# Layer 1's values and gates by seven half-size products over pairs of row tiles and column blocks, with weight operands formed and stored in layer 0

## The chip, the core and the metric

The kernel runs on one core of one Trainium2 chip. The metric is the device time of one execution, in microseconds (us). A core has a matrix engine (TensorE, in profiles PE), VectorE (DVE), ScalarE (ACT), GpSimd (POOL) and SyncE (SP), which here only issues transfers. Each engine works through its own list of instructions in order; semaphores tie the lists together. Matrix products accumulate in PSUM, everything else lives in SBUF, and DMA moves data to and from HBM.

## What is computed

A backbone of two layers over 2048 latent tokens and 256 context tokens of width 1024. Layer 0 mixes latent attention and gated linear attention; layer 1 is a 2-D neighbourhood attention. The change concerns layer 1's input projection:

```python
def odd_mixer(h, hc, w_in, q_gain, k_gain, rpb, w_out, update_ctx):
    def heads(u):
        bsz, n, _ = u.shape
        q, k, v, z = jnp.split(u, 4, axis=-1)
        sh = lambda t: t.reshape(bsz, n, C_HEADS, C_HD)
        return rms_norm(sh(q), q_gain), rms_norm(sh(k), k_gain), sh(v), z

    q_x, k_x, v_x, z_x = heads(jnp.dot(h, w_in))
    q_c, k_c, v_c, z_c = heads(jnp.dot(hc, w_in))
    o = neighborhood_attention(q_x, k_x, v_x, k_c, v_c, rpb)
    y = jnp.dot(o.reshape(h.shape[0], h.shape[1], C_WIDTH) * jax.nn.silu(z_x), w_out)
```

`w_in` is 1024 x 4096, with 1024 columns each for queries, keys, values and gates. All is in float32.

## The kernel before

**Tiles and precision.** Tokens stand in 18 row tiles of 128 (tiles 0 and 1 are context), the width in 8 blocks of 128 (`k`), the columns of layer 1's projection in 8 blocks of 512 (`j`: 0, 1 queries; 2, 3 keys; 4, 5 values; 6, 7 gates). A float32 product is made of three matmuls: every operand is split into a high part (rounded to the engine's format by an ACT copy) and a low part (the rest, by a subtraction), and high x high, high x low and low x high are summed (`mm3_steps`, L134 to L136). A *cell* is one row tile by one column block: 8 blocks of `k` x 3 = 24 matmuls of 512 columns into one PSUM bank.

**Stages.** `even_latent` and `even_rest` make layer 0's projections, `even_mix` its attention and output, `odd_qk` layer 1's queries and keys, `odd_vz` its values and gates, `odd_tail` its attention and output. `even_rest` weaves its cells with layer 0's row maxima; weights of its first blocks are split by steps in `self.ahead`, one of which `pump` issues at every fourth step of the main work.

**`odd_qk`** transposes and modulates each row tile (`prep`, `modulate`), stores it in `H` for later and runs the cells of j = 2, 3, 0, 1, three banks in turn. `fin` transposes, scales and stores a cell's result later. Whenever a column block is used up, the next stage's block is loaded and split in its place (`od_steps`: `wraw`, an ACT copy, a DVE subtraction), as steps that `turn` takes. The last three tiles run block by block, with the first value cells of j = 4 at the end; one tile's parts are kept in `HL`.

**`odd_vz`** runs the other value and gate cells, tile by tile: `reload` brings a tile from `H` and splits it again (ACT `hhi`, DVE `hlo`). A value cell is copied out by ACT (`ovz`) and stored by two GpSimd DMAs (`store_v`, L1619). A gate cell takes a tanh on ACT, a multiply-add on DVE (L1649), four transposes (L1652), an ACT copy (`ozt`) and an ACT DMA. `weave` interleaves these 24-matmul cells with `maxes`, upper bounds of each head's scores: per head 16 *items*, each a context matmul (L1704, two items share a bank and a DVE reduction, L1706) and a window matmul (L1711) that DVE adds to a bias table and reduces (L1715). After the 16 items of a head `row` transposes the result (L1668), ACT copies it (`mr`) and four GpSimd DMAs store it in `M` (L1672). Tables (`mtab`), keys (`mk`) and queries (`mq`) come by SP.

**What sets the order.** The program is written in the order that the generators give; `weave(main, side, ratio, lag, head)` takes `ratio` items for each step of the main work and ties a step to an item `lag` back. The framework then orders each engine's list by a simulated schedule, so that instructions can stand in another order than written. A tile's buffer is reused as soon as the last reader in its list is done; DMA issues wait on their queue for that, and hold back what is behind them.

**The seven products.** Layer 0's and layer 1's output projections already use this form (`seven`, L1359): for two row tiles and two column blocks, with the width cut into two halves, the four results come of seven half-width products instead of eight; sums and differences of the blocks stand in their operands, and partial sums pass from one product to the next in the same bank.

## Time and profile before

| | |
|---|---|
| median of 3 runs | 3512.95 us (3510.87 to 3515.46) |
| the profiled execution | 3515.51 us, span 3513.7 us |
| granted clock of the span | 0.994 |
| DMA traffic | 518.00 MB, mean 147 GB/s |
| stages in the span | even_rest about 555 to 1095, odd_qk about 2075 to 2507, odd_vz about 2507 to 2966 us |

Times of day in views are us from the start of the span. A row of a group has line, engine, operation, names out<-in, shapes and count, then busy time and mean length, then the engine's idle time just before and what ended it. A matmul's own length (some 0.4 us for 512 columns) includes the pipeline's depth; its cost to TensorE is the spacing to the next one. Line L111 is a helper through which all of ACT's copies go.

### The profile page before, as it was taken

The page shows a single profiled execution, that of the slowest core. Times are in us where ns is not written, and L with a number is a line of the kernel's source. Part 1 is how long each engine was busy: PE and PEld are TensorE (multiplying, and loading weights), DVE is VectorE, ACT ScalarE, POOL GpSimd, SP SyncE. Part 2 cuts the span into 40 slices and gives each one's busy share as a digit, 9 for nine tenths or more (in the row PEclk, how much of TensorE's full clock was granted, in tenths as well). Part 3 has the DMA queues.
Part 4 walks back from the last instruction along what each step waited for, and adds up shares of the span by engine and source line. Part 5 has one row for each costly group of instructions (what it writes and reads, how often), then busy time and mean ns, then how long its engine had stood idle before and what let it go on. Part 6 is the DMA issues. An engine that isn't in the chain of part 4 may idle for free.

```text
span 3513.7 us, 54120 instructions
## 1 busy us (share of the span) xinstructions
PE 3433.5 (98%) x20228; PEld 2652.7 (75%) x20228; DVE 2350.5 (67%) x3853; ACT 1466.1 (42%) x2612; POOL 1057.8 (30%) x1309
## 2 busy tenths in 40 slices
PE   8999998999999999999999999999999999999899
PEld 6898987888887666665556888888888887555577
DVE  4677756888886777768886655545576663566765
ACT  5445542111113554546664344445422222555632
POOL 1343331111111334332210123333211112787711
PEclk9999999999999999999999999999999999999999
DMA  7555555232325242333634664444766556655374
GB/s 255 144 161 159 148 141 160 96 106 81 103 81 162 62 139 71 102 115 121 179 113 122 131 172 151 152 154 144 262 185 185 179 181 207 222 191 188 120 189 62
DMA packets 354714, 518.00 MB, mean 147 GB/s; under 512 B 33178, under 2 KB 233578, under 8 KB 347492
## 3 DMA queue, kind: packets, MB, share of 16 engines
q1 hardware_dynamic: 301972, 396.55, 37.4%
q0 software_dynamic: 29456, 82.14, 8.9%
q10 hardware_dynamic: 23024, 35.85, 2.9%
q8 instruction: 159, 2.61, 0.3%
q14 instruction: 103, 0.84, 0.1%
HBM read 335.63 MB, written 196.60 MB: 151 GB/s over the span
## 4 chain that ended last, share of the span: by engine, by line
PE 83%; DVE 5%; DMA 5%; ACT 2%; issue 2%; POOL 2%; SPq 1%; ACTq 0%; DVEq 0%; POOLq 0%
PE gm L136 10%; PE gm L134 10%; PE st L1178 10%; PE gm L135 10%; PE av L1088 7%; PE mx L708 4%; PE st L1798 4%; PE o L1828 2%; PE pu L1367 2%; PE o L1367 2%; PE o L1810 1%; PE st L1367 1%; PE pj L1367 1%; PE mx L1711 1%; PE up L127 1%
## 5 line engine op out<-in xcount | busy, mean ns | idle before, releaser
L709 DVE TENSOR_REDUCE mm<-mx 128x1 f32<-128x512 f32 (+1 forms) x656 | 389.2, 628 | 85.2 <-PE mx L708 78.1
L111 ACT ACTIVATE apt<-st 128x1024 f32<-128x1024 f32 (+1 forms) x296 | 300.1, 1014 | 305.9 <-PE st L1178 285.9
L1185 DVE TENSOR_TENSOR acc<-acc,apt 128x1024 f32<-128x1024 f32 x256 | 340.7, 1331 | 83.0 <-ACT apt L111 64.3
L1178 PE MATMUL st<-aq,akh 64*128 64x512 f32 x1728 | 312.7, 410 | 1.0 <-ACT apt L111 0.6
L1088 PE MATMUL av<-apt,av 128*64 128x512 f32 x1152 | 265.8, 598 | 0.0
L708 PE MATMUL mx<-mk,mq 96*128 96x512 f32 (+1 forms) x656 | 236.1, 373 | 5.4 <-DMA mq<-QC 5.4
L1834 POOL TENSOR_TENSOR oacc<-oacc,opt 128x528 f32<-128x528 f32 (+6 forms) x192 | 220.6, 1170 | 44.6 <-ACT opt L111 40.3
L1178 PE MATMUL st<-aq,akl 64*128 64x512 f32 (+1 forms) x1152 | 230.9, 392 | 0.0
L111 ACT ACTIVATE u<-gm 128x352 f32<-128x352 f32 (+1 forms) x140 | 68.5, 496 | 374.9 <-PE gm L136 206.0
L1178 PEld LDWEIGHTS st<-aq,akh 64*128 64x128 f32 x1728 | 153.2, 186 | 83.1 <-ACT apt L111 28.0
L1980 DVE TENSOR_TENSOR opt<-st,tab 128x496 f32<-128x496 f32 (+16 forms) x288 | 124.3, 484 | 117.3 <-PE st L1798 116.9
L1715 DVE CUSTOM_DVE_ANT_0 mx<-mx,mtab 128x465 f32<-128x465 f32 (+7 forms) x256 | 137.2, 542 | 75.0 <-PE mx L1711 70.3
L1088 PEld LDWEIGHTS av<-apt,av 128*64 128x64 f32 x1152 | 76.3, 136 | 135.3 <-issue 134.3
L111 ACT ACTIVATE opt<-opt 128x930 f32<-128x930 f32 (+7 forms) x130 | 104.5, 805 | 133.0 <-DVE opt L1980 124.5
L708 PEld LDWEIGHTS mx<-mk,mq 96*128 96x128 f32 x656 | 121.7, 189 | 17.3 <-issue 5.8
L1178 PEld LDWEIGHTS st<-aq,akl 64*128 64x128 f32 (+1 forms) x1152 | 112.2, 185 | 23.9
L1706 DVE TENSOR_REDUCE mm<-mx 128x2 f32<-128x512 f32 x128 | 88.2, 689 | 45.4 <-PE mx L1704 43.6
L223 POOL TENSOR_TENSOR oss<-oss,mhalf 128x8 f32<-128x8 f32 x68 | 112.3, 1652 | 5.4
L134 PE MATMUL gm<-w1h,hhi 128*128 128x512 f32 x280 | 112.2, 401 | 0.0
L1555 DVE TENSOR_TENSOR onat<-gm,oss 128x512 f32<-128x512 f32 x68 | 46.9, 690 | 95.7 <-POOL oss L223 95.7
L136 PE MATMUL gm<-w1h,hlo 128*128 128x512 f32 x280 | 110.1, 393 | 0.0
L135 PE MATMUL gm<-w1l,hhi 128*128 128x512 f32 x280 | 109.7, 392 | 0.0
(778 smaller groups left out, 9557.0 us busy)
## 6 DMA issues: line engine op xcount, KB each, us to landing
H<-x ACTq DMA_DIRECT2D x32, 512.0 KB
adaw<-ada_w SPq DMA_DIRECT2D x64, 256.0 KB
wraw<-w_od SPq DMA_DIRECT2D x64, 256.0 KB
K1t<-okt POOLq DMA_DIRECT2D x16, 1024.0 KB, 6.6
x<-H SPq DMA_DIRECT2D x31, 512.0 KB
mtab<-rpb_q SPq DMA_DIRECT2D x16, 585.0 KB
x<-xin SPq DMA_DIRECT2D x18, 512.0 KB
x<-xin POOLq DMA_DIRECT2D x18, 512.0 KB, 5.2
```

What stands on the lines that cost most here:

```text
L111: return self.nc.scalar.activation(out, in_, func, **kw)
L134: self.nc.tensor.matmul(out, lh(k), rh(k), start=start and j == 0, stop=False)
L135: self.nc.tensor.matmul(out, lh(k), rl(k), start=False, stop=False)
L136: yield self.nc.tensor.matmul(out, ll(k), rh(k), start=False, stop=stop and j == n - 1)
L708: mm = nc.tensor.matmul(ps[:, :w], q[:A_QK, (t % 6) * P : (t % 6) * P + P], k[:A_QK, k0 : k0 + w], start=True, stop=True)
L709: nc.vector.tensor_reduce(out=m[:, t, n : n + 1], in_=ps[:, :w], axis=AX.X, op=ALU.max)
L1088: mm = nc.tensor.matmul(O[j, nb][i * 64 : i * 64 + 64, :w], V[j, kt // TT][:, kt % TT, i * 64 : i * 64 + 64], pts[:, i, :w], start=n == 0, ...
L1178: mm = nc.tensor.matmul(ps[:, o // 64, :w], k[o : o + r, kb, kq], Q[o : o + r, qb, :w], start=m == 0, stop=m == 4)
L1185: added = nc.vector.tensor_tensor(out=acc[:, :, :w], in0=a[:, :, :w], in1=pts[:, :, :w], op=ALU.add)
L1367: self.mm = self.nc.tensor.matmul(ps, x[:, k, :], y, start=start and k == 0 and n == 0, stop=k == self.H4 - 1 and n == 2, skip_group_check ...
L1798: mm = nc.tensor.matmul(ps(i), ones[s] if k is None else k[s, ks], qs(q[s]), start=n == 0, stop=n == 3)
L1834: nc.gpsimd.tensor_tensor(out=a, in0=a, in1=pts[:, :, a0 - r0 : a1 - r0, :], op=ALU.add)
```

## The change

Row tiles t and t+1, the two column blocks of the values (or of the gates) and the two halves of the width form a *unit*: 9 units of values (18 tiles) and 8 of gates (16 tiles), 7 products of 12 matmuls each.

- **Weight operands.** Seven *parts* for the values and seven for the gates (sums and differences of the blocks, split into high and low) are formed in `even_rest` by `sum_steps`, appended to `self.ahead`: per step of 256 columns 4 SP loads, 11 GpSimd operations, 7 ACT copies and 7 GpSimd stores to `Tw`, 16 times in all (176, 112 and 112; 29.4 MB are stored). The splitting of blocks 4 to 7 in layer 1 goes. `weight_part` loads a ready part (128 x 4096, 2.1 MB) into the place of a weight.
- **Row operands.** `operand(n, i)` forms the operand of product i of unit n: up to one GpSimd sum or difference, an ACT copy (high) and a GpSimd subtraction (low); 7 and 11 operations of 512 columns a unit. They are written after product i of the unit before. `pair_load` brings the two tiles from `H` by SP (three loads, 1 MB) after products 5 and 6.
- **`odd_qk`** has no value cells any more; the last two tiles run block by block, and unit 0 (values of tiles 0 and 1) at the end, with the remaining `fin`. Parts 0 to 6 of the values are loaded as slots come free: one after j = 0, two each after 1, 2 and 3. `HL` goes.
- **`odd_vz`** runs units 1 to 8 (values) and 9 to 16 (gates), woven with `maxes` at 0.64 items per step of three matmuls, head 16 (before 0.615, 32). Unit 8 loads gate part i after its product i. Three of a unit's results need a DVE addition; gates are transposed later (`flip`). `mx` has 4 banks instead of 5.

```diff
+    def sum_steps(self, f, sp):
...
+        for k in range(self.H4):
+            for c in (slice(0, 256), slice(256, 512)):
...
+                def split(n, x):
+                    y = self.tl(sp, [P, 2, 256], "tsp", F32R, bufs=2)
+                    self.act(y[:, 0, :], x[:])
+                    dif(y[:, 1:2, :].rearrange("p z c -> p (z c)"), x, y[:, 0:1, :].rearrange("p z c -> p (z c)"))
+                    g.dma_start(self.Tw[f, n, :, :, k, c], y[:].bitcast(F32))
...
@@ even_rest
+            self.ahead += [self.held(self.sum_steps(f, sp)) for f in range(2)]
...
@@ odd_qk
-            nxt = {2: 4, 3: 5, 0: 6, 1: 7}
-            done = lambda j: j in nxt and self.later.append(self.od_steps(win, nxt[j], ws, lambda: self.done))
...
+                for i in {0: (0,), 1: (1, 2), 2: (3, 4), 3: (5, 6)}[j]:
+                    self.weight_part(0, i, ws)
+                if j == 0:
+                    self.later.append(self.operand(0, i) for i in range(4))
+            cells = self.cells(list(range(NT - 2)), (2, 3, 0, 1), lambda t, j: j > 1 or t >= NCT, 1, 0)
+            cells += [(t, j) for j in range(4) for t in (NT - 2, NT - 1)]
...
+    PARTS = [(2, "h"), (3, "h"), (3, "l"), (0, "h"), (0, "l"), (1, "h"), (1, "l")]
...
+    def weight_part(self, f, i, ws):
+        n, z = self.PARTS[i]
+        x = self.pw[i] = self.tl(ws[n // 2], [P, 2, self.H4, 512], f"w{n}{z}", F32R, bufs=1)
+        self.wload = self.nc.sync.dma_start(x[:].bitcast(F32), self.Tw[f, i])
...
+    def operand(self, n, i):
...
+        if i in before:
+            o, x, y, op = before[i]
+            g.tensor_tensor(out=o, in0=x, in1=y, op=op)
+        x = (a[0], t, t, a[1], b[0], a[1], b[1])[i]
+        hi, lo = self.ops[i]
+        self.act(hi, x)
+        g.tensor_tensor(out=lo, in0=x, in1=hi, op=ALU.subtract)
+        if i > 4:
+            self.pair_load(n + 1, (i - 5,))
+    def unit(self, n, banks, place, result, ws):
...
+        for i, ps in enumerate((U, V, U, W, U, V, U)):
+            w, op = self.pw[i], self.ops[i]
+            for k in range(self.H4):
+                for m, (x, y) in enumerate(((0, 0), (0, 1), (1, 0))):
+                    mm = self.nc.tensor.matmul(ps, op[x][:, k, :], w[:, y, k, :], start=i in (0, 1, 3) and k == 0 and m == 0,
+                                               stop=k == self.H4 - 1 and m == 2, skip_group_check=True)
+                yield mm
+            if i < 3:
+                kept[(3, 4, 5)[i]] = x = place()
+                self.done = self.act(x, ps)
+            else:
+                row, c = {3: (0, 0), 4: (1, 1), 5: (0, 1), 6: (1, 0)}[i]
+                result(t + row, c, ps, kept.pop(i, None), place)
+            if swap:
+                self.weight_part(1, i, ws)
+            self.operand(n + 1, i)
...
@@ odd_vz
-            self.weave(gemms, maxes(), 0.615, 15, 32)
+            self.weave(gemms(), maxes(), 0.64, 15, 16)
```

The change moves instructions at three places that the prediction speaks of. Rows show line, operation, out<-in with the tile's numbers, shape and the semaphores waited for (lines of the changed kernel where it is its list).

TensorE in `odd_vz` before: products of a cell (`gm`) stand one to four at a time between maxes items (`mx`).

```order
L135 MATMUL gm_27092<-w3l_23682,hhi_26622 128x512
L136 MATMUL gm_27092<-w3h_23681,hlo_26623 128x512
L134 MATMUL gm_27092<-w3h_23681,hhi_26622 128x512
L1711 MATMUL mx_26925<-mk_26485,mz_4058_23643 128x288 [waits DVE_49]
L135 MATMUL gm_27092<-w3l_23682,hhi_26622 128x512
```

TensorE in `odd_vz` now, within one of the two longest bunches: between a product on part w3l (`sv` is a unit's bank, L1713 its matmul) and one on w1h stand 10 items; L1843 and L1850 are the former L1704 and L1711. This is the end of the bunch.

```order
L1843 MATMUL mx_25721<-mk_25683,mz_4218_24265 128x256 [waits DVE_49]
L1850 MATMUL mx_25723<-mk_25683,mz_4218_24265 128x352 [waits DVE_49]
L1850 MATMUL mx_25738<-mk_25683,mz_4218_24265 128x264 [waits DVE_49]
L1843 MATMUL mx_25747<-mk_25683,mz_4219_24266 128x256 [waits DVE_49,Activation_49]
L1850 MATMUL mx_25749<-mk_25683,mz_4219_24266 128x360 [waits DVE_49]
L1850 MATMUL mx_25760<-mk_25683,mz_4219_24266 128x480 [waits DVE_49]
L1713 MATMUL sv_25705<-w1h_24087,hlo_24092 128x512 [waits Activation_49]
L1807 MATMUL mx_25773<-ident_58,mc_25681 16x128 [waits DVE_49]
L1713 MATMUL sv_25704<-w3l_23901,w2l_23791 128x512 [waits Pool_49]
```

The items there used to have products between them; each now waits for DVE with no other work for TensorE in between.

SP's list in `odd_vz` before: only tables, queries, keys and reloaded tiles.

```order
L1681 DMA mtab_26710<-rpb_q 128x936 [waits DMAHW5_49,DVE_49]
L397 DMA x_27167<-H 128x1024 [waits DMAHW6_49,DVE_49]
L1681 DMA mtab_26784<-rpb_q 128x869 [waits DVE_49]
L1698 DMA mq_26869<-Q 64x512 [waits DMAHW2_49,Activation_49]
L1698 DMA mq_26938<-Q 64x512 [waits DMAHW3_49,DMAHW2_49,Activation_49]
```

SP's list in `odd_vz` now, at unit 8: the gate parts (`Tw`) w3h and w2h stand a few rows ahead; these follow.

```order
L1659 DMA w0h_26093<-Tw 128x4096 [waits PE_49]
L1684 DMA wraw_23794<-H 128x512 [waits Pool_49]
L1659 DMA w3l_26055<-Tw 128x4096 [waits DMAHW5_49,PE_49]
L1820 DMA mtab_25995<-rpb_q 128x869 [waits DMAHW6_49,DVE_49]
L1837 DMA mq_26082<-Q 64x512 [waits DMAHW7_49,Activation_49]
L1681 DMA x_23792<-H 128x1024 [waits DMAHW0_49,Pool_49]
L1659 DMA w0l_26129<-Tw 128x4096 [waits DMAHW1_49,PE_49]
L1828 DMA mk_26142<-K 128x2304 [waits DMAHW2_49]
L1659 DMA w1h_26169<-Tw 128x4096 [waits DMAHW3_49,PE_49]
L1659 DMA w1l_26209<-Tw 128x4096 [waits DMAHW4_49,PE_49]
```

Weight loads that wait for a product now stand among the tables, queries and pairs, in one queue.

TensorE at the end of `odd_vz` before: the last row's transpose (L1668, from `mc`) stands in the last gate cell, with four value cells of context tiles behind it.

```order
L134 MATMUL gm_27506<-w3h_23681,hhi_27169 128x512 [waits Activation_49]
L135 MATMUL gm_27506<-w3l_23682,hhi_27169 128x512
L1668 MATMUL mx_27368<-ident_58,mc_27366 16x128 [waits DVE_49,PE_49]
L136 MATMUL gm_27506<-w3h_23681,hlo_27170 128x512
L134 MATMUL gm_27506<-w3h_23681,hhi_27169 128x512
```

TensorE at the end of `odd_vz` now (L1807 is that transpose, L1784 `flip`, L1933 attention's first scores):

```order
L1713 MATMUL sv_28145<-w1l_26209,hhi_24093 128x512 x7
L1807 MATMUL mx_28125<-ident_58,mc_28123 16x128 [waits DVE_49,PE_49]
L1713 MATMUL sv_28145<-w1l_26209,hhi_24093 128x512 x2
L1784 MATMUL tp_28241<-ident_58,hlo_24264 128x128 [waits DVE_49,Activation_49]
L1784 MATMUL tp_28263<-ident_58,hlo_24264 128x128 [waits DVE_49,Activation_49]
L1784 MATMUL tp_28280<-ident_58,hlo_24264 128x128 [waits DVE_49,Activation_49]
L1933 MATMUL st_28359<-qh_28334,kh_28336 128x512 [waits DMAHW2_49,DMAHW0_49]
```

The transpose moved from four cells ahead of attention's scores to two matmuls and three groups of transposes ahead (three more of each group, without a wait, are not shown).

More of the change, by code (lines that the diff above doesn't have):

```diff
@@ L720, in even_rest @@
             self.weave(gemms, maxes(), 1.06, 30, 20)
+            self.drain()
     @staticmethod
@@ new lines, in odd_qk @@
+            places = [self.tl(sp, [P, 512], "oql")[:] for _ in range(2)] + [spare[:, n] for n in range(2)]
+            banks = [self.tl(pp, [P, 512], "gm", bufs=3)[:] for _ in range(3)]
+            for n, _ in enumerate(self.unit(0, banks, lambda: places.pop(0), self.value, ws)):
+                if n % 4 == 2 and pend:
+                    fin(*pend.pop(0))
+                self.turn(1)
+    PARTS = [(2, "h"), (3, "h"), (3, "l"), (0, "h"), (0, "l"), (1, "h"), (1, "l")]
+    UNITS = [(0, t) for t in range(0, NT, 2)] + [(1, t) for t in range(NCT, NT, 2)]
@@ L1608, in by_tile, with value @@
+    def value(self, t, c, ps, x, place):
+        if x is None:
+            x = place()
+            self.done = self.act(x, ps)
+        else:
+            self.done = self.nc.vector.tensor_tensor(out=x, in0=ps, in1=x, op=ALU.add)
+        self.store_v(t, c, x)
     def by_tile(self, out, in_):
@@ L1661, in odd_vz, with gemms @@
+            def gemms():
+                for n, (f, _) in list(enumerate(self.UNITS))[1:]:
+                    banks = [self.tl(pp, [P, 512], f"sv{(n + i) % 3}", bufs=1)[:] for i in range(3)]
+                    for step, mm in enumerate(self.unit(n, banks, place, (self.value, gate)[f], ws)):
+                        if step % 4 == 1:
+                            flip()
+                        yield mm
+                flip()
             zq = [[self.tl(mp, [P, 512], f"mz{i}{a}", F32R, bufs=1) for a in range(2)] for i in range(2)]
```

174 lines of the change are left out of this document (108 added, 66 removed).

## The prediction

> **What bounds the kernel now.** I read the page first (busy shares and the chain), then windows of the layer-1 stages, then groups, timelines and DMA there.
>
> ```profile
> PE 3433.5 (98%) x20228; PEld 2652.7 (75%) x20228; DVE 2350.5 (67%) x3853; ACT 1466.1 (42%) x2612; POOL 1057.8 (30%) x1309
> ...
> PE 83%; DVE 5%; DMA 5%; ACT 2%; issue 2%; POOL 2%; SPq 1%; ACTq 0%; DVEq 0%; POOLq 0%
> ```
>
> TensorE holds 83% of the chain. Three windows show where the change works: layer 0's remaining projections (600:700), layer 1's Q/K (2200:2300) and its V/Z (2600:2700). Behind the time range stand its length and each engine's busy time, then the granted clock, the DMA share and GB/s.
>
> ```profile
> 600.00:700.00 100.00, 99.90 (x521) 88.72 (x521) 79.34 (x132) 13.02 (x23) 11.82 (x21) 1.00 0.27 89
> 2200.00:2300.00 100.00, 100.00 (x490) 82.87 (x489) 50.06 (x78) 48.19 (x99) 37.01 (x45) 1.00 0.49 154
> 2600.00:2700.00 100.00, 100.00 (x502) 84.39 (x500) 66.64 (x179) 26.85 (x44) 14.38 (x26) 1.00 0.57 178
> ```
>
> In all three PE never pauses, at full clock (1.00), so matmuls that go there are worth their whole spacing, as long as nothing else becomes late. VectorE has a third of V/Z free, GpSimd 86%.
>
> **The matmuls that go.** 68 cells of 24 matmuls (1632) become 17 units of 7 products of 12 (1428); the listed order agrees: 10602 matmuls of 512 columns before, 10398 after, 204 fewer. The chain has the price of 12 and of 24 such matmuls, in the even output projection, which already uses seven products:
>
> ```profile
> 1940.10 2.80 PE pu L1367 x12
> ...
> 1951.21 5.44 PE pu L1367 x24
> ```
>
> 2.80/12 is 0.233 us, 5.44/24 is 0.227: **-47 us** (46.2 to 47.6). The 128 transposes stay. The dropped weight splits (32 on ACT, 32 on DVE) and reload splits lie under the full PE and give nothing.
>
> **Bunches of maxes.** After the change two places of the PE order hold 9 and 10 maxes items with no product between. VectorE's pace, and PE's, are in these timelines (start, length, engine, line):
>
> ```profile
> 2685.88 0.58 DVE L1715 CUSTOM_DVE_ANT_0 mx<-mx,mtab 128x372 f32<-128x372 f32 x1
> 2686.38 0.14 DVE L1715 DVE_READ_ACCUMULATOR2_ANT mm<- 128x1 f32 x1
> 2686.38 0.69 DVE L1706 TENSOR_REDUCE mm<-mx 128x2 f32<-128x512 f32 x1
> 2686.99 0.54 DVE L1715 CUSTOM_DVE_ANT_0 mx<-mx,mtab 128x372 f32<-128x372 f32 x1
> 2687.45 0.14 DVE L1715 DVE_READ_ACCUMULATOR2_ANT mm<- 128x1 f32 x1
> 2687.45 0.50 DVE L1715 CUSTOM_DVE_ANT_0 mx<-mx,mtab 128x288 f32<-128x288 f32 x1
> ```
>
> ```profile
> 2930.35 0.40 PE L1704 MATMUL mx<-mk,mz 128*128 128x256 f32 x2
> 2930.59 0.40 PE L135 MATMUL gm<-w1l,hhi 128*128 128x512 f32 x1
> 2930.82 0.39 PE L136 MATMUL gm<-w1h,hlo 128*128 128x512 f32 x1
> 2931.05 0.34 PE L1711 MATMUL mx<-mk,mz 128*128 128x384 f32 x1
> 2931.23 0.40 PE L134 MATMUL gm<-w2h,hhi 128*128 128x512 f32 x1
> ```
>
> Two items take VectorE 2687.45-2685.88 = 1.57, 0.79 each; PE needs 0.24/2+0.18, about 0.3. Ten items keep VectorE 7.9 us and PE 3. Four buffers let PE run 2 to 3 items (2 us) ahead: 3 us of stall, 5 if VectorE starts behind. Two bunches: **+8** (0 if VectorE has caught up and the products behind it are ready, 16 if each also stands behind a unit's three additions and a row's end).
>
> **The exchange of weights.** After product i of unit 8 the value part i is overwritten by gate part i: seven loads of 2.1 MB, 14.7 in all. Between them SP's order has three tables, three loads of a pair, a query and one set of keys, sized here:
>
> ```profile
> x<-H SPq DMA_DIRECT2D x31, 512.0 KB
> mtab<-rpb_q SPq DMA_DIRECT2D x16, 585.0 KB
> ...
> mk<-K SPq DMA_DIRECT2D x8, 1152.0 KB
> ```
>
> With tables of 1.5 MB together, 1.0 of the pair, 0.1 and 1.2, 18.5 MB pass until the last part. The fastest stretches of this trace, and V/Z itself, give the rate:
>
> ```profile
> 8.00:14.00 6.00, 5.83 (x18) 2.94 (x20) 0.07 (x1) 0.00 (x0) 0.00 (x0) 1.00 1.00 410
> 14.00:20.00 6.00, 6.00 (x32) 2.37 (x28) 0.17 (x1) 0.60 (x1) 0.00 (x0) 1.00 1.02 427
> 2984.00:2990.00 6.00, 6.00 (x56) 3.52 (x54) 4.24 (x5) 2.86 (x4) 4.43 (x4) 1.00 1.04 375
> ```
>
> At 400 GB/s that is 46 us, at 178/0.57 = 312 (V/Z's rate at a full share) 60. The room lies between product 1 of unit 8, which frees the first slot in SP's order, and product 6 of unit 9: 11 products of 2.8 with some 2.5 maxes items each, 39 us, and with the row ends and transposes between them about 44. With 2 to 7 us until the first byte and between queued waits: **+9** (3 to 18). Each load waits in SP's queue for its product; behind it stand tables (for VectorE) and queries (for ACT, then the maxes), late by the same time, so maxes can't fill the gap.
> The Trainium skill (DMA: Bandwidth & Descriptors, Specifications) gives a core about 358 GB/s from HBM; by it the exchange takes 52 us and costs 6 more. The rows of 410 and 427 stand above it.
>
> **Unit 0** needs parts 5 and 6 (4.2 MB), whose slots come free only when the last Q/K cell ends, 5 and 6 products (14 and 17 us) later; at 312 to 400 GB/s 11 to 14 us, with K's stores beside them: **+3** (0 to 6).
>
> **Operands.** Groups of V/Z, and two of other stages, price GpSimd (count, busy, mean ns, idle before):
>
> ```profile
> L1672 POOL DMA_DIRECT2D M<-mr x64 | 38.5, 608 | 111.8 <-ACT mr L111 110.7 <-issue 1.1
> L1619 POOL DMA_DIRECT2D V<-ovz x58 | 31.0, 538 | 243.4 <-ACT ovz L111 217.8 <-ACT mr L111 25.7
> ```
>
> ```profile
> L1013 POOL TENSOR_TENSOR rc<-rc,azt 128x512 f32<-128x512 f32 x16 | 20.6, 1290 | 129.4 <-DVE rc L1011 129.4
> L1013 POOL TENSOR_TENSOR rc<-rc,azt 128x256 f32<-128x256 f32 x4 | 4.1, 1020 | 14.3 <-DVE rc L1011 10.1 <-DMA azt<-zaT 3.0 <-DVE acc L1185 1.1
> ```
>
> A value unit has 11 additions or subtractions (11 x 1.29 = 14.2), 8 V issues (4.3) and one row's 4 M issues (2.4): 20.9 us. PE's unit is 84 x 0.233 + 18 x 0.3, about 25. GpSimd is 84% busy and just fits; an operand has nearly a unit until its use. But M issues stand among the operands in GpSimd's order, and each waits for a maxes row: **+6** (0 to 35, the upper end being the rival below, in part). Gate units have no V issues: 16.6; VectorE has there 18 x 0.79 + 7 x 0.69 = 19 of 25. The pairs' loads are 1 MB a unit where a tile's 0.5 stood for four cells, 8 MB more in some 440 us, 0.06 of share on 0.57; each waits in SP's queue for GpSimd's last use of its buffer, with queries behind it: part of the 6.
>
> **Sums in layer 0.** 176 GpSimd operations of 256 columns at 1.02 (180 us) and 112 issues, at 0.55 as the V row, 62. With 12% of 540 us busy now it becomes 57%. They stand ahead of the stores that free PE's evictions; one step (two operations and an issue, 2.6 us) is covered by PE's second accumulator (a cell of 24, 5.5 us). The traffic, 29.4 MB of stores and 8.4 of loads, adds 70 GB/s to 89, which makes the share 0.27 some 0.5. **+2** (0 to 15, a tenth of a us for each of the 128 steps, and a little).
>
> **The end.** After the change the last row's transpose stands 2 matmuls and 12 transposes ahead of attention; before, its stores had some 25 us (2940.6 to the first scores, evicted at 2967.7). The end of V/Z in the timelines of PE, ACT, GpSimd and SP, with the stores' landing:
>
> ```profile
> 2937.33 0.27 PE L1668 MATMUL mx<-ident,mc 128*16 128x128 f32 x1
> ```
>
> ```profile
> 2937.64 0.27 ACT L111 ACTIVATE mr<-mx 16x128 fp32r<-16x128 f32 x1
> ...
> 2967.72 1.94 ACT L111 ACTIVATE opt<-st 128x1024 f32<-128x1024 f32 x2 [1.31 <-PE st L1798]
> ```
>
> ```profile
> 2938.20 2.41 POOL L1672 DMA_DIRECT2D M<-mr  x4 [5.03 <-ACT mr L111]
> ```
>
> ```profile
> DMA to landing us min/median/max: 1.7/2.2/5.7
> ```
>
> ```profile
> 2944.67 0.64 SPq L116 DMA_DIRECT2D om<-M  x2
> ```
>
> From the transpose 0.9 to the issues, 2.4, landing 2.2, and about as much again for the load that the scores' fourth term needs: 8 us. PE has 0.5, three groups of transposes that each await an ACT copy (about 1.2 each) and six score matmuls: **+4** (0 to 7).
>
> **Sum**: -47+8+9+3+6+2+4 = **-15**. The profiled run took 3515.5 (span 3513.7): 3500.5, and 3498 against the median 3512.95, 2.6 below that run.
>
> **Rivals.** *All of it is hidden*: bunches find VectorE idle, loads come at 427 GB/s, and only the exchange's 3 us stay: -44, **3469**. For it: the idle shares. Against it: the loads' sum exceeds their room by rows.
> *The saving is spent on waits*: bunches and exchange at their upper ends, -47+16+18+3+6+2+4 = +2, **3515**; so also if layer 0's sums cost 15. For it: 312 GB/s is what this stage's small runs give.
> *GpSimd becomes the bound of the value units, slower than before*. One line shows an operation of the same shape at two lengths:
>
> ```profile
> L853 POOL TENSOR_TENSOR gat<-gat,ge x18: 1265/2182/2188, 1174.2 to 1595.3; 128x512 f32<-128x512 f32 x18
> ```
>
> At 2.18 a value unit costs 24.0+6.7 = 30.7 us against 25: 5.7 x 8 = 46, in place of the 6: +25, **3538**. From 1.66 us (11x+6.7 = 25) it costs time, from 2.0 it ends slower than before. Against it: the long ones lie beside VectorE's operations on two SBUF inputs (L1185), and V/Z's have one input in PSUM.
> The Trainium skill (SBUF — State Buffer, SBUF: two separate sides) has this as a rule: a VectorE operation with two SBUF inputs and a GpSimd operation lock each other out of one port pair. By it 1.29 holds in value units; the two lengths of L853 agree.
> *That it doesn't do what it says* falls: 204 matmuls are gone from the order.
>
> **Chances.** Forecast (3483 to 3506) 0.45; hidden 0.17; spent 0.23; GpSimd 0.15. A difference under 0.2% (7 us) is about what a measurement of this kernel can't tell from none. Faster by more: 0.45+0.17 = 0.62; within: 0.23; slower: 0.15. The range 3471 to 3528 leaves out part of the hidden case (0.07) and most of GpSimd's (0.12).
>
> **What would show it.** Right: PE waits in V/Z of 15 to 30 us, the largest on weight loads at unit 9 and on VectorE at the two bunches; GpSimd operations at 1.3 us; PE still full in layer 0. Wrong: PE waiting for GpSimd in every value unit, operations above 1.7 us, or layer 0's projections longer than their 540 us.

## The result, and the profile after

| | before | after |
|---|---|---|
| median, us | 3512.44 (4 runs, 3510.87 to 3515.46) | 3547.51 (4 runs, 3541.36 to 3550.17) |
| profiled execution, us | 3515.51 (span 3513.7) | 3550.17 (span 3548.4) |
| granted clock of the span | 0.994 | 0.984 |

The ratio is 1.0096, with a 95% interval of 1.0079 to 1.0114: the changed kernel is some 35 us **slower**. Forecast were 3498, 15 faster, and the range ended at 3528.

From the page of the changed kernel, the busy times and the chain's shares, first by engine and then by line:

```profile
PE 3415.1 (96%) x20024; PEld 2629.1 (74%) x20024; DVE 2349.1 (66%) x3857; ACT 1553.5 (44%) x2820; POOL 1512.8 (43%) x1784
...
PE 76%; DMA 8%; DVE 6%; issue 3%; ACT 3%; POOL 3%; SPq 1%; ACTq 0%; DVEq 0%; POOLq 0%
PE st L1214 9%; PE gm L137 7%; PE gm L136 7%; PE gm L135 7%; PE av L1124 7%; PE sv L1713 6%; PE mx L743 4%; PE st L1933 3%; DMA mq<-Q 2%; PE o L1403 2%; PE o L1963 2%; PE o L1945 1%; PE st L1403 1%; PE pu L1403 1%; PE up L128 1%
```

TensorE has 204 instructions fewer, as counted. But its share of the chain fell from 83% to 76%, that of DMA rose from 5% to 8%, and a load of 128 KB, a query (`mq`), stands there with 2%, more than any load of a weight part.

The windows of the changed kernel: range, length, then busy time and count of PE, weight loads, DVE, ACT and POOL, then the granted clock, the DMA share and GB/s. The first answers to that of before; the second is layer 1's start, with the row of the kernel before behind it; then comes V/Z to the first score.

```profile
600.00:700.00 100.00, 99.30 (x516) 87.74 (x515) 78.55 (x131) 24.14 (x52) 67.79 (x98) 1.00 0.59 189
2030.00:2140.00 110.00, 102.52 (x474) 83.84 (x473) 60.17 (x97) 52.44 (x115) 39.20 (x46) 0.98 0.74 212
```

```profile
2030.00:2140.00 110.00, 106.86 (x502) 87.53 (x501) 62.75 (x101) 53.55 (x116) 39.38 (x46) 1.00 0.70 193
```

```profile
2505.00:2535.00 30.00, 19.95 (x81) 15.40 (x80) 5.94 (x9) 9.79 (x17) 14.88 (x16) 0.89 0.87 331
2535.00:2625.00 90.00, 88.19 (x420) 73.42 (x419) 50.18 (x137) 31.27 (x56) 70.66 (x77) 1.00 0.67 216
2625.00:2655.00 30.00, 26.85 (x113) 20.48 (x112) 18.91 (x59) 10.15 (x19) 17.50 (x20) 0.89 0.71 225
2655.00:2690.00 35.00, 35.00 (x169) 29.25 (x168) 19.02 (x53) 12.19 (x22) 28.60 (x33) 1.00 0.49 139
2690.00:2706.00 16.00, 15.18 (x59) 10.73 (x58) 11.38 (x37) 4.50 (x9) 12.85 (x17) 0.89 0.73 226
2706.00:2738.00 32.00, 32.00 (x155) 26.85 (x154) 18.91 (x52) 8.97 (x17) 20.36 (x24) 1.00 0.78 286
2738.00:2782.00 44.00, 27.10 (x99) 20.86 (x98) 11.85 (x34) 11.88 (x20) 18.93 (x18) 0.73 0.90 353
2782.00:2980.00 198.00, 189.36 (x950) 157.97 (x949) 144.90 (x367) 90.48 (x162) 120.08 (x109) 0.98 0.52 159
2980.00:2997.00 17.00, 6.49 (x35) 5.07 (x34) 2.70 (x4) 4.22 (x7) 4.13 (x5) 0.82 1.00 339
```

Layer 0 carries its sums for nothing (PE 99.30 of 100, POOL at 68 where 12 stood). In V/Z there are stretches without any loss, and between them holes at the start, in two bunches, at the exchange, over the gate units and at the end. *Lost* below is the length of a stretch less what its matmuls take at the spacing that their shapes have in the full stretches. The last column repeats the forecast's terms.

| place | lost after, us | forecast |
|---|---|---|
| the matmuls that went | -47 | -47 |
| sums in layer 0 | 0 | 2 |
| start of layer 1, 2030 to 2140 | 10.8, before 4.8 | none |
| from unit 0 to unit 1, 2505 to 2535 | 12.2 | 3 |
| value units, 2535 to 2625 | 2.3 | with the gate units |
| two bunches, 2625 to 2655 and 2690 to 2706 | 8.4 and 5.5 | 8 |
| exchange, 2738 to 2782 | 24.1 | 9 |
| gate units, 2782 to 2980 | 18.0 | 6 |
| end, 2980 to 2997 | 11.9 | 4 |
| attention | 3.8 longer | none |

V/Z lost 82.7 us (7.9 before): 59.3 in pauses of PE and some 20 in matmuls at half clock (18 to 22, by how slow a matmul has to be to count). The forecast's terms for V/Z come to 30, and 82.7 - 7.9 is 74.8. -47 + 6 + 74.8 + 3.8 is 38; the spans differ by 34.7, so 3 us are placed nowhere.

**The exchange.** No product there waited for a weight part. The chain of the changed kernel and SP's timeline (start, length, queue, line, out<-in) show what was waited for:

```profile
2729.66 20.30 DMA mq<-Q
...
2750.62 21.77 DMA mq<-Q
```

```profile
2741.92 0.32 SPq L1659 DMA_DIRECT2D w1l<-Tw  x1
...
2749.31 0.32 SPq L1684 DMA_DIRECT2D wraw<-H  x1
2750.62 0.45 SPq L1837 DMA_DIRECT2D mq<-Q  x1
```

A query is issued behind parts of 2.1 MB (w1l is the last), a table and a row tile, and lands 20 us later. ACT takes its copies in order (the bracket is the idle time before, and what ended it), and PE takes the maxes in order:

```profile
2772.41 0.63 ACT L112 ACTIVATE mz<-mq 64x512 fp32r<-64x512 f32 x1 [8.57 <-DMA mq<-Q]
```

```profile
2773.10 0.58 PE L1843 MATMUL mx<-mk,mz 128*128 128x256 f32 x1 [8.23 <-ACT mz L112]
...
2774.63 1.48 PE L1713 MATMUL sv<-w0l,hhi 128*128 128x512 f32 x3
```

The product at 2774.63 was ready: three of its matmuls had run at 2763.89. What held it were six matmuls of maxes ahead of it, the first of 0.58 us. That pause of 8.23 us is the longest there; the others, 4.42, 1.67, 1.56 and 1.02 us, ended with row operands and, the last, with a copy out of a bank. Ahead of the 4.42 ACT had stood 12 us for a row tile:

```profile
2741.96 0.63 ACT L112 ACTIVATE hhi<-wraw 128x512 fp32r<-128x512 f32 x1 [12.01 <-DMA wraw<-H]
```

The 16 DMA engines had no room: over 54 us they were full.

```profile
2720.00:2774.00 54.00, 37.10 (x159) 29.35 (x158) 18.35 (x53) 12.63 (x22) 23.60 (x27) 0.83 1.01 405
```

**Half clock.** After a pause the next products run at half rate. Two windows around that landing, and two groups of six products of the same shape, at 2776 and at 2780:

```profile
2764.00:2774.00 10.00, 1.77 (x7) 1.28 (x8) 0.06 (x1) 0.63 (x1) 0.00 (x0) 0.58 0.99 372
2773.50:2779.00 5.50, 5.50 (x19) 4.62 (x19) 2.08 (x6) 0.60 (x1) 1.55 (x2) 0.50 0.54 192
```

```profile
2776.62 2.81 PE L1713 MATMUL sv<-w0l,hhi 128*128 128x512 f32 x6
...
2780.72 1.55 PE L1713 MATMUL sv<-w1h,hlo 128*128 128x512 f32 x6
```

PE is without a gap from 2773.5 to 2779 and does half the work. The page's busy time hides that: it shows in the clock column.

**The start and the end** have the same form. The waits of PE from 2480 to 2998 (total us, times, longest), and ACT's timeline at the end:

```profile
PE tp L1784 <- ACT ovz L112: 11.3, 3, 9.8
PE mx L1843 <- ACT mz L112: 9.9, 2, 8.2
PE sv L1713 <- DVE hx L1732: 6.8, 1, 6.8
```

```profile
2995.20 0.37 ACTq L1788 DMA_DIRECT2D z<-ovz  x1
2995.67 0.60 ACT L112 ACTIVATE ovz<-tp 128x512 f32<-128x512 f32 x1 [8.08 <-DMA ov<-V]
```

At 2504 a row tile of 256 KB took 18.17 us behind parts 5 and 6, with K's last stores behind it on SP. At 2986 ACT stood before a gate's store until attention's first loads had landed, and the copy behind that store freed PE's last transposes, 9.8 us later. The row of M, which the forecast followed there, was not what PE waited for.

**GpSimd** did not become the bound. One group of its operations (shortest, median, longest ns, and when):

```profile
L1699 POOL TENSOR_TENSOR w2l<-x,w2l x34: 1265/1292/1737, 2464.6 to 2951.6; 128x512 fp32r<-128x512 f32 x34
```

### The profile page after: what moved, and what is told of

It is laid out like the page before. It is cut to its first block, busy times and chain, and to the rows that moved or that the text cites. A ratio compares the mean times of both kernels' runs of the same rounds, so it can differ in the third digit from the quotient of the medians.

```text
span 3548.4 us, 54931 instructions
## 1 busy us (share of the span) xinstructions
PE 3415.1 (96%) x20024; PEld 2629.1 (74%) x20024; DVE 2349.1 (66%) x3857; ACT 1553.5 (44%) x2820; POOL 1512.8 (43%) x1784
## 4 chain that ended last, share of the span: by engine, by line
PE 76%; DMA 8%; DVE 6%; issue 3%; ACT 3%; POOL 3%; SPq 1%; ACTq 0%; DVEq 0%; POOLq 0%
PE st L1214 9%; PE gm L137 7%; PE gm L136 7%; PE gm L135 7%; PE av L1124 7%; PE sv L1713 6%; PE mx L743 4%; PE st L1933 3%; DMA mq<-Q 2%; PE o L1403 2%; PE o L1963 2%; PE o L1945 1%; PE st L1403 1%; PE pu L1403 1%; PE up L128 1%
## 5 line engine op out<-in xcount | busy, mean ns | idle before, releaser
L222 POOL TENSOR_SCALAR sqk<-sqk 128x8 f32<-128x8 f32 x36 | 13.3, 368 | 210.9 <-DVE sqk L559 155.6
L112 ACT ACTIVATE x<-px,modB,modA 128x128 f32<-128x128 f32 x264 | 96.3, 469 | 14.6 <-PE px L364 12.0
L1933 PEld LDWEIGHTS st<-qh,kh 64*128 64x128 f32 x384 | 36.7, 185 | 86.2 <-issue 36.1
```

The lines of the kernel that those rows point to most:

```text
L112: return self.nc.scalar.activation(out, in_, func, **kw)
L1933: mm = nc.tensor.matmul(ps(i), ones[s] if k is None else k[s, ks], qs(q[s]), start=n == 0, stop=n == 3)
```

## The experiments

All are edits of the changed kernel. Ratios are to the kernel before, run beside them, with 95% intervals; the change itself stands at 1.0096.

**Without the exchange (e1).** The gates are computed with the values' parts:

```diff
-            if swap:
-                self.weight_part(1, i, ws)
```

> The changed kernel without the seven loads of gate parts in unit 8: the gate units multiply with the value parts (14.7 MB of loads and the right gates are left out). Theory A (bulk loads at the exchange hold up what is queued behind them, and TensorE with it): of the 61 us of TensorE gaps in V/Z the 18 us between 2739 and 2773 go, and about 5 us of matmuls at half clock behind them: some 3525 us against 3547. Rival (VectorE's pace in the bunches of maxes, or GpSimd's operands, are what stops TensorE): the gaps stay or move, within 5 us of 3547.

3524.78, 1.0027 (1.0016 to 1.0039): 0.69% or 24 us below the change. The window of the exchange in this kernel:

```profile
2738.00:2782.00 44.00, 41.17 (x200) 32.69 (x198) 30.68 (x87) 18.55 (x33) 28.82 (x28) 1.00 0.61 194
```

PE has 200 matmuls there where 99 stood, at full clock. By the table's reckoning unit 8 and unit 9 together lose 5 us here and 24.5 in the change; most of the rest of the 24 came from the gate units behind, which take 27.3 us each where 28.8 stand in the change. So the exchange accounts for some 20 us. But this kernel is still 10 us above the kernel before, with 47 us of matmuls less: 57 lie in other places.

**Half the bytes (e6).** Gate parts bring their high half only, and it serves as low half too:

```diff
-        self.wload = self.nc.sync.dma_start(x[:].bitcast(F32), self.Tw[f, i])
+        self.wload = self.nc.sync.dma_start(x[:, : 2 - f].bitcast(F32), self.Tw[f, i][:, : 2 - f])
...
-... op[x][:, k, :], w[:, y, k, :], ...
+... op[x][:, k, :], w[:, y * (1 - f), k, :], ...
```

> The changed kernel with only the high halves of the gate parts loaded in unit 8 (7.3 MB of loads left out; the gates' high x low matmuls use the high half in its place, as many matmuls as before). Volume theory: 11 MB fit the room of 44 us, no gap is left at the exchange, as with no loads at all: 3525 us. Order theory (a small load waits for whole parts ahead of it): waits halve, gaps of 6 to 9 us remain: 3533 to 3537.

3528.57, 1.0034 (1.0018 to 1.005), with every load still in its place in the queue.

```profile
2738.00:2782.00 44.00, 38.19 (x186) 30.66 (x186) 25.42 (x70) 21.12 (x37) 32.61 (x31) 1.00 0.75 271
```

Unit 8 and unit 9 lose 4.5 us, no more than without any loads. So it is the bytes that pass in these 50 us, not the number of loads or the waits for their slots.

**Another queue for the queries (e2).**

```diff
-                            nc.sync.dma_start(q[b : b + 64].bitcast(F32), ...
+                            nc.scalar.dma_start(q[b : b + 64].bitcast(F32), ...
```

> The changed kernel with the 64 query loads (128 KB) issued from ScalarE's queue in place of SyncE's, nothing left out. If the order in a queue is the matter (a query load lands only when the 2.1 MB loads issued ahead of it on the same queue have landed, 20 us at the exchange): the 8.4 us gap at 2764 goes, ScalarE's waits for queries fall from 101 us to under half, 3530 to 3538 us. If the sheer volume at the exchange is the matter: gaps stay at 2739 to 2773, 3543 to 3550 us.

3548.18, 1.0101 (1.0072 to 1.0131): nothing gained. The query no longer waits, but the pair's load does, ACT with it, and PE with ACT (10.1 us):

```profile
2766.51 1.15 ACT L112 ACTIVATE w2l<-x 128x512 fp32r<-128x512 f32 x2 [16.75 <-DMA x<-H]
```

**Rows and queries on other queues (e5)**: this edit, and `pair_load` issued by GpSimd.

> The changed kernel with the row tiles' loads (1 MB a unit) issued by GpSimd and the queries by ScalarE; SyncE's queue keeps the weight parts, tables and keys; nothing left out. With the queries alone moved the gap only changed places: TensorE then waited 10 us for a row operand, whose tile (0.5 MB) landed 17 us late behind the parts. If the order in the queue is the matter (small loads behind big ones), both kinds now pass the parts: the exchange's gaps fall from 18 to under 8, 3532 to 3538 us. If the volume is (18.5 MB in some 44 us), TensorE waits as long, now for the parts themselves: 3543 to 3550.

3557.57, 1.0114 (1.0077 to 1.0151), no better: with both out of SP's queue PE waited for keys at the exchange, 4.8 us, and shorter waits lay all over the stage.

**K's last stores by ACT (e3)** for the last two row tiles, so that they don't stand behind parts 5 and 6:

```diff
-                    nc.sync.dma_start(self.K1[j0 : j0 + 4, ...
+                    (nc.scalar if t >= NT - 2 else nc.sync).dma_start(self.K1[j0 : j0 + 4, ...
```

> The changed kernel with the key stores (K) of the last two row tiles issued from ScalarE's queue, not behind the loads of weight parts 5 and 6 in SyncE's. Theory A: ScalarE no longer waits 20 us for those stores to free its buffer, the 7 us gap at the start of unit 1 (2523) shrinks to at most 2, with 1.5 us at half clock: about 3539 us. Rival (unit 1 waits for its row tiles' own loads, which landed 18 us after issue behind the same parts): the gap stays at 5 or more, 3545 us.

3544.95, 1.0092 (1.0063 to 1.0121). Its waits of PE at unit 1's start, 6.8 in the change:

```profile
PE sv L1713 <- DVE hx L1732: 3.6, 1, 3.6
```

Half of that wait was the stores; the total is within the interval of the change.

**The gates' stores by GpSimd (e4).**

```diff
-                    nc.scalar.dma_start(self.z1[c * 4 : c * 4 + 4, ...
+                    nc.gpsimd.dma_start(self.z1[c * 4 : c * 4 + 4, ...
```

> The changed kernel with the gates' 32 z stores issued by GpSimd, not by ScalarE, nothing left out. Theory A (at the end ScalarE's store issue waits for one of attention's first loads, its copies of transposed gates stand behind it, and TensorE behind those): the 10 us gap at 2986 falls to 2 to 5, where the last row of maxima sets the start of attention; 3538 to 3542 us. Rival (GpSimd is the bound of these units): 32 issues more make gate units longer, 3550 us or more.

3544.86, 1.0082 (1.0059 to 1.0105). The wait at the end went, as its waits of PE from 2970 to 2998 show (9.8 before the edit):

```profile
PE tp L1784 <- ACT ovz L112: 2.4, 2, 1.7
```

Two new pauses in the gate units, 2.5 and 3.6 us, took some of it back. The profiled execution is the fastest of three; their median is 3 us below that of the change, within the intervals.

**All of these together (e7)**, with GpSimd's stores for the last two tiles only:

> Three moves at once, nothing left out: row tiles by GpSimd and queries by ScalarE, the last key stores by ScalarE, the last two tiles' z stores by GpSimd. If each removes its own wait and none gives it back: 8 to 10 us at the exchange, 3 to 8 at unit 1, 8 at the end, 3520 to 3530 us. If waits removed come back elsewhere (ScalarE and GpSimd as holders of the operands): 3540 or more.

3554.8, 1.0106 (1.007 to 1.0142). No gain. By the table's reckoning the exchange, the gate units (25.9 us each) and both ends lost less, but units 1 to 6 lost some 33 us, where 10 stood. Why they did wasn't tried.

**Two buffers for queries (e9)**, against the bunches:

```diff
-                            q = self.tl(mp, [P, 512], "mq", F32R, bufs=1)
+                            q = self.tl(mp, [P, 512], "mq", F32R, bufs=2)
```

> The changed kernel with two buffers for queries in place of one, so that a quarter's load is issued a quarter earlier; nothing left out. Theory B (ScalarE waits 101 us for queries, the operands' high copies stand behind those waits): waits for queries fall under 50 us, the losses in the bunches (14 us) and in the gate units (18 us) fall by 8 to 12 together: about 3537 us. Rival (VectorE's pace in the bunches, the turn of gate results in the gate units): both keep their losses within 4 us, 3543 to 3550.

3540.28, 1.0075 (1.0049 to 1.0102). The pauses of the bunches shrank and a gate unit came to 26.9 us; exchange and half clock stayed.

**The queries' copies on VectorE (e13)**, with those two buffers:

```diff
-        self.act(out.rearrange("d (c r b) -> d r c b", c=4, r=8), ...
+        self.nc.vector.tensor_copy(out.rearrange("d (c r b) -> d r c b", c=4, r=8), ...
```

> The changed kernel with two query buffers and the 64 copies of queries made by VectorE, so that ScalarE never waits for a query; nothing left out. If ScalarE's in-order waits are the coupling: 5 to 10 us under the run with two buffers alone (3540), 3530 to 3535. If the coupling sits in VectorE as much (it waits in ScalarE's place, with the results' additions and the maxes behind it): within 4 us of 3540 or above it.

3558.52, 1.0144 (1.0121 to 1.0168), the slowest of those that compute everything. ACT is now free of the queries, but DVE's own reductions stand behind the copies: PE waited 11.3, 7.0 and 3.6 us for DVE, and 15.1 for keys at the exchange. Another engine that takes its work in order is no way out here.

**The units alone (e12)**: no exchange, and the maxes after all units instead of between them:

```diff
-            self.weave(gemms(), maxes(), 0.64, 15, 16)
+            for mm in gemms():
+                pass
+            side = maxes()
+            while True:
+                with self.tc.issue_after(mm.ins):
+                    if next(side, self) is self:
+                        break
```

> The changed kernel with all units first and the maxes after them, not woven, and without the loads of gate parts (the right gates are left out). The 256 items then stand alone and take VectorE 0.79 us each, some 125 us more in all; what is read is the stretch of the 17 units alone. If the operands (ScalarE's high copies and GpSimd's subtractions) bound a unit by themselves: over 21 us a unit (GpSimd 18.5 to 20.9 us against 84 matmuls in 19.5). If the weaving with the maxes is what costs (ScalarE, VectorE and SyncE shared with them): 19.5 to 20.3 us a unit, no pause over 1 us after unit 1, and no matmul at half clock.

3728.6 (one run); what counts is the pace. Two windows of the units, values and then gates, and the first products of gate units 10 and 16:

```profile
2560.00:2660.00 100.00, 95.38 (x411) 76.14 (x410) 10.37 (x15) 32.40 (x57) 87.29 (x95) 1.00 0.38 108
2720.00:2840.00 120.00, 102.55 (x450) 81.45 (x448) 24.28 (x30) 45.49 (x79) 67.26 (x52) 0.94 0.29 84
```

```profile
2720.02 0.62 PE L1713 MATMUL sv<-w2h,w2l 128*128 128x512 f32 x2
...
2880.76 1.52 PE L1713 MATMUL sv<-w2h,w2l 128*128 128x512 f32 x6
```

A gate unit takes (2880.76 - 2720.02)/6 = 26.8 us, a value unit 21.1 (units 1 to 7), and the 84 matmuls of either 19.5. So a gate unit alone takes longer than the 25 us that the forecast gave to the unit *with* its maxes; a value unit doesn't. What the gate unit waits for, the timelines of GpSimd, ACT and PE show in one unit:

```profile
2786.48 1.26 POOL L1695 TENSOR_TENSOR wraw<-wraw,wraw 128x512 f32<-128x512 f32 x1 [3.35 <-DMA wraw<-H]
```

```profile
2787.78 0.63 ACT L112 ACTIVATE w2l<-wraw 128x512 fp32r<-128x512 f32 x1 [0.89 <-POOL wraw L1695]
...
2788.80 0.59 ACT L112 ACTIVATE ovz<-sv 128x512 f32<-128x512 f32 x1
```

```profile
2789.44 4.29 PE L1713 MATMUL sv<-w3l,w2l 128*128 128x512 f32 x12 [2.54 <-ACT ovz L112]
```

The row tile lands late; GpSimd's sum waits for it, ACT's copy for the sum, the copy that frees the bank stands behind that, and PE waits for the bank. All waits of PE for such copies from 2480 to 2860:

```profile
PE sv L1713 <- ACT ovz L112: 18.6, 11, 4.6
```

**The rows earlier (e14)**: the second row tile has two buffers, and is loaded after product 2 instead of 6:

```diff
-        if i > 4:
-            self.pair_load(n + 1, (i - 5,))
+        if i == 5:
+            self.pair_load(n + 1, (0,))
+        if i == (2 if n > 1 else 6):
+            self.pair_load(n + 1, (1,))
...
+            self.alt = [self.tl(sp, [P, self.H4, P], "rb", bufs=2) for _ in range(2)]
```

> The changed kernel with a second pair of buffers for the upper row tile, loaded five products earlier from unit 3 on; nothing left out. Theory C (just in time: the row tile lands after the unit's first product, GpSimd's sum and ScalarE's copy of it wait, and the copy that frees a bank waits behind them, 27 us a gate unit even with no maxes beside it): gate units, 28.8 us each now, fall to under 27.5, the loss there from 18 to under 10 us, and the exchange loses some us because this tile is ahead of the parts: 3530 to 3538 us. Rival (the row tiles are not what the copies wait for): within 4 us of 3547.

**Six places for results (e15)** instead, so that a bank is copied out sooner:

```diff
-            place = lambda: self.tl(sp, [P, 512], "ovz", bufs=4)[:]
+            place = lambda: self.tl(sp, [P, 512], "ovz", bufs=6)[:]
```

> The changed kernel with six result buffers in place of four; nothing left out. Rival to theory C (a gate's buffer is held until its z store has landed, and the next unit's copies wait for it): gate units fall under 27.5 us, 3535 to 3540 us. Theory C: they stay at 28 to 29, within 4 us of 3547.

e14: 3541.58, 1.0076 (1.0059 to 1.0093). e15: 3551.08, 1.0105 (1.0088 to 1.0122). The first products of units 10 and 16, of e14 and then of the change:

```profile
2794.73 0.62 PE L1718 MATMUL sv<-w2h,w2l 128*128 128x512 f32 x2
...
2952.52 0.84 PE L1718 MATMUL sv<-w2h,w2l 128*128 128x512 f32 x3
```

```profile
2787.27 1.54 PE L1713 MATMUL sv<-w2h,w2l 128*128 128x512 f32 x6
...
2959.98 0.85 PE L1713 MATMUL sv<-w2h,w2l 128*128 128x512 f32 x3
```

A woven gate unit: 28.8 us in the change, 26.3 with early rows, and 28.4 with more places (the same products at 2791.57 and 2961.72). More places change little. The row's landing sets part of the pace, but not alone: with two query buffers (e9) the same six units took 26.9 us each, with the queries on ACT's queue (e2) 27.3, both with the rows where the change has them. By the table's reckoning these six units lose 16.7 us in the change, 8.6 in e14, 8.3 in e9 and 8.1 in e2; the rest of the difference in pace is work that the order places outside them. The intervals of e14 and of the change overlap, so its gain of 6 us in the median is not clear of noise.

**The copies to the output later (e8).** Without the tie of the former order, sixteen copies of 512 KB (`out<-x1`) had moved from V/Z into layer 1's start. This ties them back:

```diff
-                    nc.scalar.dma_start(self.out[o : o + P, :], ...
+                    with self.tc.issue_after(self.done.ins):
+                        nc.scalar.dma_start(self.out[o : o + P, :], ...
```

> The changed kernel with the 16 copies of the stream to the output (512 KB each) tied to a gate result again; in the changed kernel nothing ties them, and the framework's order had put them into layer 0's end and layer 1's first projections. Theory: their traffic is what makes TensorE lose 8 to 11 us instead of 5 between 2030 and 2140; with them late this loss falls to 5 (4 to 5 us gained), and up to that much comes back beside the exchange and the gate units: 3541 to 3547 us. Rival (the loss there comes of the changed order of loads of layer 1's weights): the loss stays at 8 to 11.

3558.24, 1.0126 (1.0102 to 1.0151). The start's loss was 8.6 then, where 10.8 stood, and V/Z became worse. In that window PE was busy for 105.6 us, and for 106.5 and 106.0 in e10 and e11 below, which have this tie too; in the runs without it the profiles show 102.4 to 105.3. So the copies may be a part of that loss, but the run doesn't confirm the 5 us that were expected, and its cause stays open.

**Several together (e10)**: e3, e8, e9, GpSimd's stores for the last two tiles, and the gates' transposes two steps later (`step % 4 == 3`); **e11** is e10 without the exchange.

> Five repairs at once, nothing left out: output copies late, two query buffers, the last key stores by ScalarE, the last two tiles' z stores by GpSimd, gates transposed two steps later. If the losses outside the exchange are waits of these kinds: 4 at the start of layer 1, 3 at unit 1, 8 at the end, 5 to 10 in between, 3520 to 3527 us, the 24 us of the exchange left. If they only change places, 3540 or more.

> The same five repairs without the seven loads of gate parts (gate units multiply with the value parts, so the right gates are left out): what the change could be worth without the exchange. Additive theory: the exchange's 23 us less than the run with the repairs, 3497 to 3504 us, faster than before (3513). Rival (losses change places, half clock behind every pause): 3515 to 3525, no faster than before.

3536.89, 1.0076 (1.0047 to 1.0104), and 3527.57, 1.0042 (1.0024 to 1.006). The mends are not additive: without the exchange the kernel with them is no faster than the one without (e1, 3524.78). The pause at the end stayed at 7.7: ACT now stood there before a copy to the output.

**Early rows and the two ends (e16)**: e14, e3 and GpSimd's stores for the last two tiles; **e17** is e16 without the exchange.

> The early row tiles together with the last key stores by ScalarE and the last two tiles' z stores by GpSimd, nothing left out: the best of what was found without touching the exchange. Theory C and additive: 3518 to 3528 us. If losses change places: 3530 or more.

> The same three repairs without the loads of gate parts (the right gates are left out), the bound for this form with the exchange free. Theory C and additive: the run without the exchange alone (3525) less 8 to 18, 3505 to 3516 us. If losses change places: 3520 or more, as with the other repairs (3528).

3534.16, 1.0058 (1.0041 to 1.0075), and 3516.39, 1.0009 (1.0 to 1.0019). At the exchange of e16 PE waits for a load that is now the last one, the keys:

```profile
PE mx L1849 <- DMA mk<-K: 14.8, 1, 14.8
```

So even with the exchange for nothing and these waits mended, the form has just come back to the time of before.

**Keys a head earlier (e18)**: e16 with `mk` issued one head ahead.

```diff
+                    if b and j < 7:
+                        key()
...
-                        if b == 0:
-                            k = self.tl(mp, [P, T], "mk", F32R, bufs=2)
-                            nc.sync.dma_start(k[:].bitcast(F32), self.K1[j])
+                        if h == 0:
+                            key()
+                        k = keys[j]
```

> The three repairs (early row tiles, last key stores by ScalarE, last z stores by GpSimd) and the maxes' keys loaded one head earlier, so that the set needed at the exchange is ahead of the gate parts in SyncE's queue; nothing left out. With the three repairs TensorE waits 15 us at the exchange for that set (1.2 MB) and for nothing else. If the order in the queue is the matter there: that pause shrinks to under 5 us, 3534 falls to 3520 to 3526. If the volume is: the pause comes back on a part or a row tile, within 4 us of 3534. Neither gives a kernel faster than before (3514).

3527.67, 1.0044 (1.0027 to 1.006), the best version with all of its work. Its exchange in the waits of PE:

```profile
PE mx L1857 <- ACT mz L112: 16.0, 2, 15.6
```

It is the query's turn again. V/Z still lost 60.3 us. No version that computes everything beat the kernel before.

## Why the prediction was wrong

**Right**: the matmuls (204 fewer at the same spacing, -47) and layer 0, whose sums cost even less than the 2 forecast. GpSimd's operations stayed at a median of 1.29 us, so the rival of 2.18 falls; that its 3538 lies nearest to the result is chance. The rule that was weighed there (the Trainium skill, SBUF — State Buffer, SBUF: two separate sides) agrees with the median of 1292 ns; that the lock was what made the long operations of before was not tried.

**The exchange: the wait was the wrong one.** The rate was right: 405 GB/s measured, 400 taken. The measured rate is above the 358 GB/s a core that the Trainium skill (DMA: Bandwidth & Descriptors, Specifications) states. The step that failed is the wait: "Each load waits in SP's queue for its product; behind it stand tables (for VectorE) and queries (for ACT, then the maxes), late by the same time", priced as what the loads overrun their room by, with PE's largest waits there expected on weight loads at unit 9. No product of unit 9 waited for a part. With the engines full, a small load lands only behind the bytes ahead of it: 128 KB took 20.30 and 21.77 us. The maxes in PE's order then hold products that are ready, and late row tiles hold others. Half the bytes took 22 us off the total (1.0096 to 1.0034), no loads 24; with the query, the rows or the keys moved, PE waited for the next one in line: 10.1 us for a row operand (e2), 14.8 for keys (e16), 16.0 for queries (e18). The exchange measured 24.1 where 9 stood, with 18 as the upper end.

**Unit 0: 12 instead of 3.** The two parts were counted, what stands behind them was not: a row tile (18.17 us) and K's stores. e3 took half of the longest wait away.

**Operands: the wrong resource.** The step compared GpSimd's sum (20.9 us in a value unit, 16.6 in a gate unit) with PE's 25 and called it a fit. For value units that came out: 2.3 us lost in the window behind the first, and 21.1 us a unit in e12. For gate units it didn't, because a sum of busy time says nothing on a chain: row tile, GpSimd sum, ACT copy, copy out of the bank, product. e12 shows it at 26.8 us for a gate unit without any maxes. Early rows take 8 us off what six woven gate units lose (e14), and so do queries on another queue or with a second buffer (e2, e9). Row operands, queries and copies out of the banks share ACT's list; which of them sets the pace was not separated. The exchange was as dear in e14 as before: PE's longest wait there became 15.5 us, for keys, where 8.2 stood.

**Bunches**: VectorE's pace was there, the size was 13.9 for 8. About half of the 13.9 is half clock, which no term had, and the longest single pause, 2.14 us, was for a row operand on ACT (last section).

**The end: 12 instead of 4.** The last row of M was followed as the late one; late was ACT, before a gate's store. e4 shows that.

**What no term had**: the half clock (some 20 us of V/Z), which makes each pause dearer than its length, layer 1's start (+6, open) and attention (+3.8, of which the runs show only that it varies: 547 to 553 us with the change). Without those 20 the result would be near 3528, the end of the range; that is an estimate from the table.

The terms also were added as if each were alone. e7, e10 and e11 show the opposite: waits mended together don't save the sum of what each cost. The reading that fits is that the stage's engines take their lists in order and share the copies of ACT, so that a wait that is mended lets another one come to the fore; only some of these followers were traced (e2, e5, e14, e16, e18).

## What to carry to other kernels

A stage in which TensorE never pauses can owe that to a lead: the loads, copies and reductions of all its strands arrive early. A change that gives it a burst of loads or a chain from load to product spends that lead, and the idle shares of the engines don't show it. Price a burst by the landing time of the smallest load that stands behind it and of what is held up in order behind that, not by the overrun of the burst itself. Add to each pause of several us the slow products that follow it, and read the chain of one unit, not its sums.

## What the runs showed of the hardware

The clock. In the change some 20 us of V/Z went to matmuls at half clock. The window from 2773.5 to 2779, above, has PE full at a clock of 0.50, for 5.5 us after a pause of 8.23. A long pause isn't needed: in a bunch of maxes it fell as well. Two windows of the changed kernel, and the product behind the bunch:

```profile
2640.00:2643.00 3.00, 2.54 (x8) 1.29 (x8) 3.00 (x11) 0.63 (x1) 1.39 (x3) 0.94 0.51 125
2643.00:2646.00 3.00, 1.18 (x3) 0.57 (x2) 2.36 (x10) 0.88 (x2) 0.00 (x0) 0.50 0.79 212
```

```profile
2646.32 1.22 PE L1713 MATMUL sv<-w1h,hlo 128*128 128x512 f32 x2 [2.14 <-ACT hlo L112]
```

The Trainium skill (TensorE: Matmul & The Clock Gate, Part 1: The HAM clock gate) has a state of half clock after an idle window of about 3.4 us, and as much sustained work until the clock is full again. The half rate and a recovery of this order agree with the rows. The fall in the bunch doesn't follow that rule as it stands: the clock is at 0.50 from 2643 on, the pause of 2.14 us began only at 2644.18, and from 2640 to 2643 PE was busy for 2.54 of 3 us, in 8 matmuls, with VectorE busy throughout.
